# Moving the tiles that TensorE reads from 32 past a multiple of 64 bytes to a multiple of 64 bytes

## The chip, the cores and the metric

The kernel runs on one core of one Trainium2 chip. The metric is the device time of one execution in microseconds; the kernel before takes 1710.17 us, the median of three runs between 1709.99 and 1710.79. A core has TensorE (matrix products, from the on-chip memory SBUF into the accumulators PSUM), VectorE, ScalarE, GpSimd, and queues that start DMA transfers. SBUF has 128 partitions; a tile has an address (its first byte) that is the same in all of them.

## The reference

One layer of a hybrid encoder on 256 tokens of 2048 features, in float32. Cut to what matters:

```python
h = rms_norm(x, norm_mix_pre)
z = h @ w_in                                   # 2048 -> 14800 columns
o_conv, o_gla, o_diff, o_rwkv = four_mixers(z) # 512 features each
gates = sigmoid(z_gate)                        # four times 2048
merged = sum(gates[n] * (o[n] @ w_branch[n]) for n in range(4))
x = x + rms_norm(merged @ w_out, norm_mix_post)
h = rms_norm(x, norm_ffn_pre)
ffn = (silu(h @ w_gate) * (h @ w_up)) @ w_down # 5632 wide
x = x + rms_norm(ffn, norm_ffn_post)
```

## The kernel before

All large products are done in float32r, a float32 whose lower bits are rounded away, in three products that together keep the precision of float32: both operands are split into a rounded part `hi` and an exact remainder `lo`, and the sum is hi x hi + hi x lo + lo x hi.

Weights come in chunks of 256 rows by 512 columns, stored as [128, 2, 512], 0.5 MB each, in the order in which they are used. `Stream.chunk` (L578) issues the load into one of 4 slots `raw` of a ring (L583), lets ScalarE cast it to `hi` (L585) and VectorE subtract to `lo` (L586), each of which has 3 slots. The load of a chunk waits until the slot that it takes is free.

A product has a stationary operand, which is loaded into the array (its weight load is listed as PEld) and a moving operand, whose columns stream through it. Four kinds of loops make them:

- `gemm_tok` (L631, products at L646 to L648): the activations are stationary, 128 features by 128 tokens, and 512 columns of weights move. For each chunk 2 halves k, 2 token tiles i and 3 products: 12. The stationary tile is `hT_hi` or `hT_lo` (the input of the layer, L674, 16 blocks of 256 columns), `oT` (the output of a mixer, L748), `mT_hi`, `mT_lo` (the merged branches, L899) or `h2_hi`, `h2_lo` (the input of the feed-forward part, in the place of `hT`, L935; named `h_hi`, `h_lo` in the profile).
- `gemm_feat` (L654, products at L666 to L668): the weights are stationary, 128 columns of a chunk at a time, and 256 tokens of `hT` move. For each chunk 2 halves, 4 column tiles and 3 products: 24. The first projection (the low-rank parts) takes chunks of 464 columns in tiles that begin at column 0, 112, 208 and 336 and are 112, 96, 128 and 128 wide.
- the down projection (L1019 to L1026): as `gemm_tok`, with `ah` and `al` stationary, split from `aT` on the way (L1009 to L1014). For its last four chunks the split weights go to `wl`, which takes the place of `hT` once more (L1037).
- the mixers' own small products (RWKV, gated linear attention, differential attention) are in plain float32, as are the transposes (L1000 and others).

The order of the work on each engine is set by a scheduler from the program order and priorities; weights have a high priority.

Tiles are placed one behind the other in pools. A pool's tiles begin at a multiple of 32 bytes. The pool `base` holds small tables and the next pool, the ring, begins behind it. The built program places the tiles as follows (first byte; in brackets modulo 64 and modulo 512):

```
raw   19616 (32, 160) + 4096 n       hi  36000 (32, 160) + 4096 n      lo  48288 (32, 160) + 4096 n
hT_hi 60576 (32, 160)                hT_lo 76960 (32, 160)             h2, wl in the same place
oT    133088, 137184, 141280, 145376 (32, 480)
mT_hi 149472 (32, 480)               mT_lo 165856 (32, 480)
ah    191712 (32, 224) + 2048 n      al  197856 (32, 224) + 2048 n
```

The blocks within a tile are multiples of 512 bytes apart, so that a stationary block has its tile's place modulo 512. In `gemm_feat` the first projection's column tiles begin 0, 448, 832 and 1344 bytes into a half, which places them at 160, 96, 480 and 480 modulo 512. Tiles of the RWKV mixer are 4128 bytes apart (64 x 64 + 32), so that every second one is a multiple of 64: the product of L300 reads `KBT` and `W` both at 32 modulo 64 in its first two rounds over the sequence, and both at 0 in the third.

Of the kernel before, what the change touches and what calls it, by code (L numbers as in the profile page):

```python
# [6 lines left out]
F32 = mybir.dt.float32  # L7
F32R = mybir.dt.float32r
# [4 lines left out]
PSUM = bass.MemoryType.PSUM  # L13

# columns of the per-feature vector table
# [60 lines left out]
def rwkv_mixer(e, Zr, Zk, Zv, Zl, wa, g2, out_hi, out_lo):  # L76
    """Z*: [128, 4, 257] feature-major projections with a zero column in front."""
# [18 lines left out]
    # token shift  # L96
    zm = {}
    for q, (n, Z) in enumerate((("l", Zl), ("k", Zk), ("r", Zr), ("v", Zv))):
        t = m4("zm_" + n)
# [12 lines left out]
    # decay, in-context rate, gate  # L112
# [31 lines left out]
    # normalised key direction  # L144
# [22 lines left out]
    # k' = k (1 + (a - 1) k_a)  # L167
# [7 lines left out]
    # bonus  # L175
# [8 lines left out]
    # scaled operands, [b | k] and [a | r] side by side within a chunk  # L184
# [12 lines left out]
    # value, token-major, under the rows of sa  # L197
# [14 lines left out]
    # intra-chunk products, transposed: rows [b s | k s], columns [a t | r t]  # L212
# [17 lines left out]
    # N = (I - U)^-1 of the 32 strictly upper 64 x 64 blocks U = AM[b rows, a columns]  # L230
# [43 lines left out]
    # chunks  # L274
# [4 lines left out]
    for c in range(4):  # L279
# [8 lines left out]
        X = e.M.tile([128, 8, 64], F32, tag="X", name="X", bufs=2)  # rows of sa; of the output  # L288
# [23 lines left out]
        # group norm per head  # L312
# [36 lines left out]
def split_out(e, ps, gain, hi, lo):  # L349
    """hi + lo <- ps * gain (per partition), hi rounded to float32r."""  # L350
    e.nc.scalar.activation(hi, ps, AF.Copy, scale=gain)  # L351
    e.nc.vector.scalar_tensor_tensor(lo, ps, gain, hi.bitcast(F32), op0=ALU.mult, op1=ALU.subtract)


def head_norm_out(e, po, i, mul, ot, scale4):
    """ot[:, i] <- po / rms over each head of 128 (times mul, token-major)."""
    nc = e.nc
    V, S = nc.vector, nc.scalar
    sq = e.T_.tile([128, 512], F32, tag="hsq", name="hsq")
    # a square beyond float32 makes the mean infinite and rsqrt zero; scaled by 2^-8 it stays finite here  # L360
    V.tensor_scalar(sq, po, 2.0 ** 64, -(2.0 ** 64), op0=ALU.min, op1=ALU.max)
    S.activation(sq, sq, AF.Square, scale=2.0 ** -8)
    st = e.T_.tile([128, 4], F32, tag="hst", name="hst", bufs=2)
    ok = e.T_.tile([128, 4], F32, tag="hok", name="hok", bufs=2)
    V.tensor_reduce(st, sq.rearrange("p (h x) -> p h x", h=4), axis=AX.X, op=ALU.add)
    top = FMAX * 2.0 ** -16
    V.tensor_scalar(ok, st, top, None, op0=ALU.is_le)
    V.tensor_scalar(st, st, top, 2.0 ** 16 * scale4 / 128.0, op0=ALU.min, op1=ALU.mult)
    V.tensor_scalar(st, st, scale4 * 1e-5, None, op0=ALU.add)
    e.nc.gpsimd.tensor_tensor(st, st, e.mhalf.to_broadcast([128, 4]), op=ALU.pow)  # L370
    V.tensor_tensor(st, st, ok, op=ALU.mult)
    for h in range(4):
        s = slice(h * 128, (h + 1) * 128)
        if mul is not None:
            V.scalar_tensor_tensor(ot[:, i, s], po[:, s], st[:, h:h + 1], mul[:, i, s], op0=ALU.mult, op1=ALU.mult)
        else:
            S.activation(ot[:, i, s], po[:, s], AF.Copy, scale=st[:, h:h + 1])
# [14 lines left out]
def gla_mixer(e, q, k, wl, v, g, wa2, out_hi, out_lo):  # L392
    """q (scaled), k: [128, 2, 256] feature-major; wl: [16, 256]; v, g: [128, 2, 512] token-major."""
# [15 lines left out]
    # log(1 + x) = 2 atanh(x / (2 + x))  # L409
# [13 lines left out]
    # scores, transposed [s, t]: within a tile of 128 [hh, i, j], and from tile 0 to tile 1 [hh, j]  # L423
# [3 lines left out]
    # the diagonal: q . k of each token and head  # L427
# [12 lines left out]
    # pairs whose halves of a block of 2w differ, scaled about the middle of the block  # L440
# [59 lines left out]
def diff_mixer(e, q, k, v, lq, out_hi, out_lo):  # L500
    """q (scaled), k: [128 (map, d), 4 heads, 256] feature-major; v: [128, 2, 512]; lq: [128, 4, 64]."""
# [49 lines left out]
def conv_mixer(e, cu, b, rB, y, out_hi, out_lo):  # L551
    """cu: [128, 4, 258] (C * u behind two zero columns), b: two banks [128, 2, 256], rB [128, 256] their factor; y: [128, 4, 256] scratch."""
    nc = e.nc
    V, S = nc.vector, nc.scalar
    o = VCOL["conv"][0]
    for ft in range(4):
        w = [e.vec[:, o + 4 * j + ft:o + 4 * j + ft + 1] for j in range(3)]
        V.tensor_scalar(y[:, ft], cu[:, ft, 0:256], w[0], None, op0=ALU.mult)
        V.scalar_tensor_tensor(y[:, ft], cu[:, ft, 1:257], w[1], y[:, ft], op0=ALU.mult, op1=ALU.add)
        V.scalar_tensor_tensor(y[:, ft], cu[:, ft, 2:258], w[2], y[:, ft], op0=ALU.mult, op1=ALU.add)  # L560
    for p in range(2):
        V.tensor_tensor(y[:, 2 * p:2 * p + 2], y[:, 2 * p:2 * p + 2], b[p], op=ALU.mult)
        V.tensor_tensor(y[:, 2 * p:2 * p + 2], y[:, 2 * p:2 * p + 2], rB.unsqueeze(1).to_broadcast([128, 2, 256]), op=ALU.mult)
    S.copy(out_hi, y)
    V.tensor_tensor(out_lo, y, out_hi.bitcast(F32), op=ALU.subtract)


# blocks of 512 columns of w_in as chunks() of it holds them
# [3 lines left out]
class Stream:  # L572
    """Weights in: DMA -> (rounded part, exact remainder), both float32r."""
# [4 lines left out]
    def chunk(self, ap, w=512, into=None):  # L578
        """ap: [128, 2, w] in DRAM -> hi, lo [128, 2, w]."""
        e, nc = self.e, self.e.nc  # L580
        with e.tc.high_priority(offset=e.boost):
            raw = self.ring.tile([128, 2, 512], F32, tag="raw", name="raw", bufs=e.nraw)
            nc.sync.dma_start(raw[:, :, :w], ap)  # L583
            hi, lo = into or [self.ring.tile([128, 2, 512], F32R, tag=t, name=t, bufs=e.nhi) for t in ("hi", "lo")]
            nc.scalar.copy(hi[:, :, :w], raw[:, :, :w])  # L585
            nc.vector.tensor_tensor(lo[:, :, :w], raw[:, :, :w], hi[:, :, :w].bitcast(F32), op=ALU.subtract)  # L586
        return hi, lo


def hybrid_kernel(tc, x, xt, w_l, w_in, w_branch, w_out, w_gate, w_up, w_down, post_mix, post_ffn, wa2_d, w2_d, a2_d, g2_d, lq_d,  # L590
# [9 lines left out]
    with ExitStack() as ctx:  # L600
# [25 lines left out]
        def rms(ssum, n, eps):  # L626
            """ssum [128, 1] <- (ssum / n + eps) ** -0.5"""
            V.tensor_scalar(ssum, ssum, 1.0 / n, eps, op0=ALU.mult, op1=ALU.add)  # L628
            G.tensor_tensor(ssum, ssum, e.mhalf.to_broadcast(list(ssum.shape)), op=ALU.pow)  # L629

        def gemm_tok(w, lhs, nk, banks, pairs=()):  # L631
            """banks[i] [128 tokens, 512] <- lhs.T @ 512 columns; w(kc) -> [128, 2, 512], lhs(kt) -> (hi, lo) [128, 256].

            Token tile 0 goes through both chunks of a pair before token tile 1 does."""
# [19 lines left out]
        def gemm_feat(src, w, tiles, banks, before=None):  # L654
            """banks[j // 2][:, j % 2] [features, 256] <- (h @ w).T by column tiles (start, width) of the chunk."""
# [18 lines left out]
        hT_hi = hpool.tile([128, 16, 256], F32R, tag="hT_hi", name="hT_hi")  # L674
        hT_lo = hpool.tile([128, 16, 256], F32R, tag="hT_lo", name="hT_lo")
# [23 lines left out]
        def x_norm():  # L699
            """The norm's factor of each token: rst by partitions, rB along the free axis."""  # L700
# [23 lines left out]
        with ExitStack() as mctx:  # L724
# [22 lines left out]
            def out_pair(tag):  # L747
                return [PB.tile([128, 4, 256], F32R, tag=tag, name="oT", bufs=2) for _ in range(2)]  # L748
# [26 lines left out]
            oT_rwkv = out_pair("oR")  # L775
            with ExitStack() as rctx:
# [7 lines left out]
                # keeps the tensor engine at work until x is there  # L784
# [112 lines left out]
            L = mctx.enter_context(tc.tile_pool(name="L", bufs=1))  # L897
            tp = mctx.enter_context(tc.tile_pool(name="tp", bufs=1, space=PSUM))
            mT_hi = L.tile([128, 16, 256], F32R, name="mT_hi")  # L899
            mT_lo = L.tile([128, 16, 256], F32R, name="mT_lo")  # L900
# [9 lines left out]
            def merged(g):  # L910
                """Features g * 512.. of the gated sum."""
# [23 lines left out]
            h2_hi = hpool.tile([128, 16, 256], F32R, tag="hT_hi", name="h2_hi")  # L935
            h2_lo = hpool.tile([128, 16, 256], F32R, tag="hT_lo", name="h2_lo")
# [42 lines left out]
        with ExitStack() as fctx:  # L979
# [27 lines left out]
            for hf in range(2):  # L1007
                bk = [[(bank() if j == 0 else wd.tile([128, 512], F32, tag="wd", name="wd", bufs=4)) for i in range(2)] for j in range(2)]
                def activations(kc):  # L1009
                    ah = F.tile([128, 2, 256], F32R, tag="ah", name="ah", bufs=3)  # L1010
                    al = F.tile([128, 2, 256], F32R, tag="al", name="al", bufs=3)
# [23 lines left out]
                if hf == 1:  # L1035
                    # of the last four chunks token tile 0 is done first
                    wide = [hpool.tile([128, 16, 256], F32R, tag=t, name="wl").rearrange("p (c k x) n -> p c k (x n)", c=4, k=2)  # L1037
# [31 lines left out]
class TagPool:  # L1069
    """A pool whose tags have a fixed number of slots."""  # L1070
# [30 lines left out]
def chunks(w, n=512):  # L1101
    """[K, N] -> [K / 256, N / n, 128, 2, n]: the pieces that the kernel loads, each in one run."""
    k = w.shape[0]
    return w.reshape(k // 256, 2, 128, -1, n).transpose(0, 3, 2, 1, 4)
# [32 lines left out]
```

## Time and profile before

| what | us |
|---|---|
| runs: median (lowest, highest) | 1710.17 (1709.99, 1710.79) |
| span of the profiled execution, first to last instruction | 1707.7 |
| TensorE busy in it | 1665.4 |
| VectorE busy | 987.1 |
| ScalarE busy | 753.0 |
| 548 subtractions to `lo` on VectorE | 686.6 |
| 548 casts to `hi` on ScalarE | 575.7 |

The durations that the profile gives for products overlap: a product of 512 columns is listed with about 390 ns, and the next one starts before it ends. How fast TensorE goes is therefore read from the distance between starts, in the timeline or in the chain of work. The weight load of the next product starts 2 to 4 ns after a product does.

### The profile page before, as it was taken

The numbers are of one execution on the slowest core, as the hardware profiler recorded it, in microseconds if no ns is written. First come the engines' busy times: TensorE is split into PE (matmuls) and PEld (weight loads), VectorE is DVE, ScalarE is ACT, GpSimd is POOL, SyncE is SP. The second block draws the span as 40 slices with busy tenths as digits, with TensorE's granted clock in tenths as the row PEclk, the third lists the DMA queues.
The fourth block names the chain that finished last, engine by engine and source line by source line (L and its number), as shares of the span: only waits on it lengthen the run. The fifth ranks groups of instructions, "written<-read, shape, count | busy, mean of one in ns | idle before, by whom it ended". The sixth has DMA issues, their size and how long they took to land. (4 is left out here: it accounts for less than half of the span.)

```text
span 1707.7 us, 21846 instructions
## 1 busy us (share of the span) xinstructions
PE 1665.4 (98%) x8630; PEld 1402.6 (82%) x8630; DVE 987.1 (58%) x1040; ACT 753.0 (44%) x873; POOL 190.0 (11%) x168
## 2 busy tenths in 40 slices
PE   7999998999999999999999899999999999999997
PEld 6999976897788987888888788888888888888886
DVE  7667644669764458545554655445455554556555
ACT  3444342335544335544444644444444444445443
POOL 4005192111210001201000100000000000000001
PEclk8999998999999999999999999999999999999999
DMA  6654445445446554765555466565565555555653
GB/s 210 201 182 136 146 161 153 141 136 185 148 149 196 186 174 161 257 196 186 185 185 185 150 209 193 187 188 193 187 197 187 190 191 186 184 190 184 194 186 134
DMA packets 86087, 306.84 MB, mean 180 GB/s; under 512 B 9713, under 2 KB 12033, under 8 KB 85473
## 3 DMA queue, kind: packets, MB, share of 16 engines
q1 hardware_dynamic: 84208, 298.50, 54.4%
q0 software_dynamic: 1200, 5.90, 1.1%
q8 instruction: 67, 1.10, 0.3%
q10 hardware_dynamic: 576, 1.05, 0.2%
q14 instruction: 36, 0.29, 0.0%
HBM read 302.40 MB, written 3.01 MB: 179 GB/s over the span
## 5 line engine op out<-in xcount | busy, mean ns | idle before, releaser
L586 DVE TENSOR_TENSOR lo<-raw,hi 128x1024 fp32r<-128x1024 f32 (+1 forms) x556 | 699.2, 1259 | 597.3 <-ACT hi L585 596.6
L585 ACT CAST hi<-raw 128x1024 fp32r<-128x1024 f32 (+1 forms) x556 | 583.4, 1050 | 759.6 <-PE mm L648 532.4
L647 PE MATMUL mm<-lo,h_hi 128*128 128x512 f32 x704 | 275.0, 391 | 0.4 <-DVE lo L586 0.4
L648 PE MATMUL mm<-hi,h_lo 128*128 128x512 f32 x704 | 274.0, 390 | 0.0
L647 PE MATMUL mm<-lo,hT_hi 128*128 128x512 f32 x608 | 240.9, 396 | 13.3 <-DVE lo L586 13.2
L646 PE MATMUL mm<-hi,h_hi 128*128 128x512 f32 x704 | 250.2, 391 | 0.5 <-ACT h_hi L351 0.5
L648 PE MATMUL mm<-hi,hT_lo 128*128 128x512 f32 x608 | 238.9, 393 | 0.0
L646 PE MATMUL mm<-hi,hT_hi 128*128 128x512 f32 x608 | 221.7, 393 | 0.0
L668 PE MATMUL mm<-hT_hi,lo 128*128 128x256 f32 (+2 forms) x640 | 183.1, 289 | 10.3 <-DVE lo L586 10.3
L666 PE MATMUL mm<-hT_hi,hi 128*128 128x256 f32 (+1 forms) x640 | 185.2, 290 | 1.8 <-ACT hi L585 1.8
L667 PE MATMUL mm<-hT_lo,hi 128*128 128x256 f32 (+1 forms) x640 | 184.2, 289 | 0.0
L647 PEld LDWEIGHTS mm<-lo,h_hi 128*128 128x128 f32 x704 | 132.2, 188 | 28.0 <-DVE lo L586 0.9
L646 PEld LDWEIGHTS mm<-hi,h_hi 128*128 128x128 f32 x704 | 132.2, 188 | 27.8 <-ACT h_hi L351 0.7
L648 PEld LDWEIGHTS mm<-hi,h_lo 128*128 128x128 f32 x704 | 132.2, 188 | 27.0
L647 PEld LDWEIGHTS mm<-lo,hT_hi 128*128 128x128 f32 x608 | 114.8, 189 | 40.0 <-DVE lo L586 15.4
L646 PEld LDWEIGHTS mm<-hi,hT_hi 128*128 128x128 f32 x608 | 114.7, 189 | 24.4
L648 PEld LDWEIGHTS mm<-hi,hT_lo 128*128 128x128 f32 x608 | 114.8, 189 | 23.7 <-issue 0.3
L668 PEld LDWEIGHTS mm<-hT_hi,lo 128*128 128x128 f32 (+2 forms) x640 | 123.8, 194 | 11.5 <-DVE lo L586 11.2
L666 PEld LDWEIGHTS mm<-hT_hi,hi 128*128 128x128 f32 (+1 forms) x640 | 124.5, 194 | 3.2 <-ACT hi L585 2.2
L667 PEld LDWEIGHTS mm<-hT_lo,hi 128*128 128x128 f32 (+1 forms) x640 | 124.3, 194 | 1.1 <-issue 0.2
L629 POOL TENSOR_TENSOR s1f<-s1f,mhalf 128x1 f32<-128x1 f32 x2 | 1.1, 540 | 721.1 <-DVE s1f L628 721.1
L767 POOL TENSOR_TENSOR acc<-acc,gt 128x512 f32<-128x512 f32 x24 | 41.5, 1748 | 332.2 <-DVE gt L766 332.2
(351 smaller groups left out, 1892.5 us busy)
## 6 DMA issues: line engine op xcount, KB each, us to landing
raw<-in_w_in_dram SPq DMA_DIRECT2D x224, 512.0 KB, 3.5
raw<-in_w_gate_dram SPq DMA_DIRECT2D x88, 512.0 KB, 3.5
raw<-in_w_up_dram SPq DMA_DIRECT2D x88, 512.0 KB, 3.5
raw<-in_w_down_dram SPq DMA_DIRECT2D x88, 512.0 KB, 3.5
raw<-in_w_branch_dram SPq DMA_DIRECT2D x32, 512.0 KB, 3.5
raw<-in_w_out_dram SPq DMA_DIRECT2D x32, 512.0 KB, 3.5
raw<-in_w_l_dram SPq DMA_DIRECT2D x8, 464.0 KB, 5.8
xs<-in_x_dram POOLq DMA_DIRECT2D x1, 2048.0 KB, 12.9
```

The costliest lines, as they stand in the source:

```text
L585: nc.scalar.copy(hi[:, :, :w], raw[:, :, :w])
L586: nc.vector.tensor_tensor(lo[:, :, :w], raw[:, :, :w], hi[:, :, :w].bitcast(F32), op=ALU.subtract)
L629: G.tensor_tensor(ssum, ssum, e.mhalf.to_broadcast(list(ssum.shape)), op=ALU.pow)
L646: mm(banks[i_], ah[:, ts], hi[:, k, :], start=kt == 0, stop=False)
L647: mm(banks[i_], ah[:, ts], lo[:, k, :], start=False, stop=False)
L648: mm(banks[i_], al[:, ts], hi[:, k, :], start=False, stop=kt == nk - 1)
L666: mm(ps, hi[:, k, cs], hT_hi[:, kt, :], start=first, stop=False, skip_group_check=True)
L667: mm(ps, hi[:, k, cs], hT_lo[:, kt, :], start=False, stop=False, skip_group_check=True)
L668: mm(ps, lo[:, k, cs], hT_hi[:, kt, :], start=False, stop=last, skip_group_check=True)
L767: G.tensor_tensor(cs, cs, gt[:, i], op=ALU.add)
```

## The change

A constant `LINE = 64` is added, and the tiles below ask for a start at a multiple of it. Comments are taken out, and the lines from the import block on stand one further down. The instructions, their order on each engine, their shapes and their waits are the same.

```diff
+LINE = 64
...
-            raw = self.ring.tile([128, 2, 512], F32, tag="raw", name="raw", bufs=e.nraw)
+            raw = self.ring.tile([128, 2, 512], F32, tag="raw", name="raw", bufs=e.nraw, align_bytes=LINE)
...
-            hi, lo = into or [self.ring.tile([128, 2, 512], F32R, tag=t, name=t, bufs=e.nhi) for t in ("hi", "lo")]
+            hi, lo = into or [self.ring.tile([128, 2, 512], F32R, tag=t, name=t, bufs=e.nhi, align_bytes=LINE) for t in ("hi", "lo")]
...
-        hT_hi = hpool.tile([128, 16, 256], F32R, tag="hT_hi", name="hT_hi")
-        hT_lo = hpool.tile([128, 16, 256], F32R, tag="hT_lo", name="hT_lo")
+        hT_hi = hpool.tile([128, 16, 256], F32R, tag="hT_hi", name="hT_hi", align_bytes=LINE)
+        hT_lo = hpool.tile([128, 16, 256], F32R, tag="hT_lo", name="hT_lo", align_bytes=LINE)
...
-                return [PB.tile([128, 4, 256], F32R, tag=tag, name="oT", bufs=2) for _ in range(2)]
+                return [PB.tile([128, 4, 256], F32R, tag=tag, name="oT", bufs=2, align_bytes=LINE) for _ in range(2)]
```

`mT_hi`, `mT_lo`, `h2_hi`, `h2_lo`, `ah`, `al` and `wl` get the same argument. The built program then places the tiles so (first byte; in brackets modulo 64 and modulo 512):

```
raw   19648 (0, 192) + 4096 n        hi  36032 (0, 192) + 4096 n       lo  48384 (0, 256) + 4096 n
hT_hi 60672 (0, 256)                 hT_lo 77120 (0, 320)              h2, wl in the same place
oT    133248, 137344 (0, 128), 141504, 145600 (0, 192)
mT_hi 149696 (0, 192)                mT_lo 166144 (0, 256)
ah    191872 (0, 384) + 2048 n       al  198080 (0, 448) + 2048 n
```

## Rows read from the trace of the kernel before

**Rows 1.** The page, busy time: engine, us, share of the span, instructions

```profile
PE 1665.4 (98%) x8630; PEld 1402.6 (82%) x8630; DVE 987.1 (58%) x1040; ACT 753.0 (44%) x873; POOL 190.0 (11%) x168
```

**Rows 2.** Who waited for whom on TensorE: us in total, times, longest

```profile
PE mm L647 <- DVE lo L586: 13.7, 5, 10.3
PE mm L668 <- DVE lo L586: 10.3, 4, 5.5
```

**Rows 3.** The same for the load queue SPq

```profile
SPq L583 <- DVE lo L586: 1397.7, 542, 16.1
```

**Rows 4.** Groups by shape, whole span: count | busy us, mean ns | idle before us

```profile
L586 DVE TENSOR_TENSOR lo<-raw,hi 128x1024 fp32r<-128x1024 f32 x548 | 686.6, 1254 | 592.7 <-ACT hi L585 592.1
L585 ACT CAST hi<-raw 128x1024 fp32r<-128x1024 f32 x548 | 575.7, 1051 | 750.6 <-PE mm L648 532.4 <-PE mm L667 129.9 <-PE mm L1026 56.9
```

**Rows 5.** Groups by shape on TensorE, one of the three products each

```profile
L647 PE MATMUL mm<-lo,h_hi 128*128 128x512 f32 x704 | 275.0, 391 | 0.4 <-DVE lo L586 0.4
L647 PE MATMUL mm<-lo,hT_hi 128*128 128x512 f32 x608 | 240.9, 396 | 13.3 <-DVE lo L586 13.2
L1025 PE MATMUL mm<-lo,ah 128*128 128x512 f32 x168 | 66.2, 394 | 0.0
L1025 PE MATMUL mm<-wl,ah 128*128 128x512 f32 x8 | 3.2, 394 | 0.0
L647 PE MATMUL mm<-lo,mT_hi 128*128 128x512 f32 x128 | 50.7, 396 | 0.0
L667 PE MATMUL mm<-hT_lo,hi 128*128 128x256 f32 x608 | 174.2, 287 | 0.0
```

**Rows 6.** The chain of work, gate and up projections: start us, us, what

```profile
1055.77 0.66 PE tq L1000 x6
...
1100.22 0.66 PE tq L1000 x6
```

**Rows 7.** The chain of work, down projection

```profile
1459.85 0.47 PE wd L1024 x2
...
1465.45 0.47 PE wd L1024 x2
```

**Rows 8.** Timeline of TensorE, output projection: start us, us, instruction, count

```profile
885.29 0.63 PE L646 MATMUL mm<-hi,mT_hi 128*128 128x512 f32 x2
...
890.89 0.39 PE L646 MATMUL mm<-hi,mT_hi 128*128 128x512 f32 x1
```

**Rows 9.** Timeline of TensorE, a feature-major projection

```profile
150.00 0.28 PE L666 MATMUL mm<-hT_hi,hi 128*128 128x256 f32 x1
...
150.96 0.28 PE L668 MATMUL mm<-hT_hi,lo 128*128 128x256 f32 x1
```

**Rows 10.** Timeline of TensorE, the first projection at full clock

```profile
38.88 0.28 PE L666 MATMUL mm<-hT_hi,hi 128*128 128x256 f32 x1
...
39.90 0.28 PE L666 MATMUL mm<-hT_hi,hi 128*128 128x256 f32 x1
```

**Rows 11.** Timeline of TensorE, the first projection near the start

```profile
13.65 0.41 PE L666 MATMUL mm<-hT_hi,hi 128*128 128x256 f32 x1
...
14.29 0.41 PE L666 MATMUL mm<-hT_hi,hi 128*128 128x256 f32 x1
```

**Rows 12.** Stretches of TensorE: us, busy (count), granted clock, DMA share, GB/s

```profile
12.00:15.00 3.00, 3.00 (x16) 0.50 1.03 401
38.50:41.00 2.50, 2.50 (x24) 1.00 0.57 203
1056.50:1099.00 42.50, 42.50 (x189) 1.00 0.62 188
```

**Rows 13.** The page, what the DMA moved in 40 slices, GB/s

```profile
GB/s 210 201 182 136 146 161 153 141 136 185 148 149 196 186 174 161 257 196 186 185 185 185 150 209 193 187 188 193 187 197 187 190 191 186 184 190 184 194 186 134
```

**Rows 14.** Timeline of TensorE, float32 products of the RWKV mixer, two places

```profile
303.00 1.16 PE L300 MATMUL ps<-W,KBT 128*128 128x128 f32 x8
...
348.19 1.16 PE L300 MATMUL ps<-W,KBT 128*128 128x128 f32 x8
```

More of the change, by code (lines that the diff above doesn't have):

```diff
@@ L898, in hybrid_kernel @@
             tp = mctx.enter_context(tc.tile_pool(name="tp", bufs=1, space=PSUM))
-            mT_hi = L.tile([128, 16, 256], F32R, name="mT_hi")
-            mT_lo = L.tile([128, 16, 256], F32R, name="mT_lo")
+            mT_hi = L.tile([128, 16, 256], F32R, name="mT_hi", align_bytes=LINE)
+            mT_lo = L.tile([128, 16, 256], F32R, name="mT_lo", align_bytes=LINE)
             xs = L.tile([128, 2, 2048], F32, name="xs")
@@ L934, in hybrid_kernel @@
             x2 = acc
-            h2_hi = hpool.tile([128, 16, 256], F32R, tag="hT_hi", name="h2_hi")
-            h2_lo = hpool.tile([128, 16, 256], F32R, tag="hT_lo", name="h2_lo")
+            h2_hi = hpool.tile([128, 16, 256], F32R, tag="hT_hi", name="h2_hi", align_bytes=LINE)
+            h2_lo = hpool.tile([128, 16, 256], F32R, tag="hT_lo", name="h2_lo", align_bytes=LINE)
             def residual(g, i, pool):
@@ L1009, in activations @@
                 def activations(kc):
-                    ah = F.tile([128, 2, 256], F32R, tag="ah", name="ah", bufs=3)
-                    al = F.tile([128, 2, 256], F32R, tag="al", name="al", bufs=3)
+                    ah = F.tile([128, 2, 256], F32R, tag="ah", name="ah", bufs=3, align_bytes=LINE)
+                    al = F.tile([128, 2, 256], F32R, tag="al", name="al", bufs=3, align_bytes=LINE)
                     S.copy(ah, aT[:, 2 * kc:2 * kc + 2])
@@ L1035, in hybrid_kernel @@
                 if hf == 1:
-                    wide = [hpool.tile([128, 16, 256], F32R, tag=t, name="wl").rearrange("p (c k x) n -> p c k (x n)", c=4, k=2)
+                    wide = [hpool.tile([128, 16, 256], F32R, tag=t, name="wl", align_bytes=LINE).rearrange("p (c k x) n -> p c k (x n)", c=4, k=2)
                             for t in ("hT_hi", "hT_lo")]
```

## The prediction

> **What bounds the kernel now.** I read the share of busy time first, then who waited for whom, then the costliest groups by shape, and last the chain of work and the timeline, to get from how long an instruction lasts to how far apart two of them start. TensorE is busy 98% of a span of 1707.7 us, VectorE 58%, ScalarE 44% [rows 1]. TensorE's longest waits, 13.7 and 10.3 us in 5 and 4 places, are for the low halves of the weights that VectorE makes, and they lie at the start [rows 2]. Everywhere else the weights wait for TensorE: the queue that loads them stands 1397.7 us in total behind VectorE's release of a slot of the ring [rows 3], and the cast that makes a high half had 750.6 us of idle time before it, 532.4 of them ended by a product that gave a slot back; a chunk costs VectorE 1254 ns and ScalarE 1051 ns [rows 4], against about 2.7 us of TensorE for the 12 products of that chunk. So the time is the number of large products times the distance between their starts.
>
> The number: each of the three products of a split has as many as the row that stands for it, so there are 3 x (704 + 608) = 3936 products of 512 columns with `hT` or `h2` as stationary operand, 6 x (168 + 8) = 1056 of the down projection, and 3 x 128 = 384 each with `mT` and `oT`. Of 256 columns, with the weights stationary and `hT` moving, there are 3 x 608 = 1824 with 128 stationary columns [rows 5] and, by the loop over its four column tiles, 96 with 112 or 96; 192 of these 1920 belong to the first projection. That is 7680 in all.
>
> The distance is not the duration in those rows (390 ns), which overlaps the next product; it is read between starts. In the gate and up projections a group of 192 products and 8 transposes comes every 44.45 us [rows 6]; six of the transposes take 0.66 us there, 110 ns each, so a product has (44.45 - 0.88) / 192 = 226.9 ns; on the timeline the starts are 226 or 227 apart. In the down projection 24 products take 5.60 us, 233.3 ns each [rows 7], in the output projection also 5.60 us for 24 [rows 8]. In the feature-major products 8 take 0.96 us, 120 ns each [rows 9]; in the first projection, whose weights lie elsewhere in their slot, 9 take 1.02 us, 113.3 ns [rows 10].
>
> Against one column per cycle of 2.4 GHz (the granted clock is 1.00 in the stretches looked at [rows 12]), 213.3 ns for 512 columns and 106.7 for 256, these are too long by 13.3, 20, 20, 13.3 and 6.7 ns. Within the reading all are whole multiples of 6.67 ns, the time of 16 columns, and 16 columns of four bytes are 64 bytes. Near the start, while the granted clock is 0.50 (1.2 GHz) [rows 12], 3 products of 256 columns take 0.64 us, 213 ns each [rows 11]: one column per cycle with nothing on top. So the excess is not work of the array; it appears when the array asks for four bytes per partition every 0.42 ns, and it comes in pieces of 64 bytes. In all it is 3936 x 13.33 + 1824 x 20 + 1728 x 13.33 + 192 x 6.67 ns = 113.3 us, 7% of the span, and the operands' addresses are the only thing that differs between the 226.9 and the 233.3 ns (same shapes, same moving buffers).
>
> **The change, part by part.** It adds no instruction and moves none: the same instructions stand in the same order on each engine. What changes is where tiles start: the ring, `hT`, `h2`, `oT`, `mT`, `ah`, `al` and `wl` all start 32 bytes past a multiple of 64 before, and on a multiple after.
>
> *The products.* A moving operand of 512 columns is 2048 bytes: 32 pieces of 64 bytes if it starts on one, 33 if it starts half-way. If TensorE reads whole pieces of 64 bytes and can have one per 6.67 ns, the 33rd costs exactly one of the steps seen, 256 columns have 17 instead of 16 and pay the same step, and at 1.2 GHz, where a piece is due every 13.3 ns, the extra one is free. That is all three observations, and the smallest excess of any row, one step in [rows 10], is what the crossing alone would give. The second and third step are then meetings of the two streams (the weight load of the next product starts with a product and reads beside it), which depend on both addresses. I take one step per product for the change and leave the meetings as they are: 7680 x 6.67 ns = 51.2 us. From this goes what does not pay the step: the products at 1.2 GHz and those that stand behind a wait, about 250 by the starts on the timeline, 1.6 us. Sum: -49.6 us. Nothing becomes late behind it: a chunk would take TensorE 12 x 220 = 2.64 us, still twice VectorE's 1.25, and 0.5 MB in that time is 199 GB/s, where a slice of this trace holds 257 [rows 13].
>
> The bounds of that term. From above (no gain): the float32 products of the RWKV mixer have both kinds of address in this trace. Eight products of 128 columns take 1.16 us with both operands 32 past a multiple of 64 (at 303.00) and 1.16 us with both on a multiple (at 348.19) [rows 14]; so at that pace alignment is worth 0. They stream a column in two cycles, where a piece is due every 13.3 ns, so by the mechanism above they should show nothing, but they bound it at zero all the same. From below: all 113.3 us, or what is left of it if each product keeps the 3.3 ns that a transpose in [rows 6] has over 106.7 ns: 113.3 - 7680 x 3.3 ns = 88.0 us. I take the one step because the row nearest to it is [rows 10], the same products with one step of excess and no more.
>
> *Other users of the moved tiles.* ScalarE's casts, VectorE's subtractions and the loads into the ring touch the same tiles at the new addresses. They end ahead of TensorE by the waits of [rows 3, 4], so I cost them at nothing; if a cast and a subtraction each became 10% slower, a chunk would need 1.16 + 1.38 us in a row against 2.64, still hidden. The ring's growth moves all later tiles by 96 to 288 bytes, which swaps both kinds of address among the float32 tiles: 0 by [rows 14].
>
> The profiled execution's own time is the span of 1707.7 us; the median of the runs, 1710.17, is 2.5 us above it for what lies around. 1707.7 - 49.6 + 2.5 = 1660.6 us.
>
> **The Trainium skill against this.** Two alignments show one cost [rows 14]. The Trainium skill, SBUF — State Buffer, section Specifications (TRN2), gives lines of 16 bytes and asks for at least two hits in each; 32 past a multiple of 64 is a multiple of 16, and every operand here is contiguous. By that rule no operand crosses more lines after than before and the time stays 1710; whether a float32r operand at full pace obeys it no row shows, since none in this trace is aligned. It is the first rival below, which stands on [rows 14] without it.
>
> **Rivals.**
> *No change.* The step is fixed per product or depends on something else than the offset within 64 bytes. For it: [rows 14]. Against it: a fixed cost would not differ between [rows 9] and [rows 10], where a product has the same moving tiles and 128 stationary columns. Time 1710, within 0.2% (3.4 us, about what measurements of this kernel can tell from no change).
> *Slower: the streams meet more often.* What counts is the distance, modulo 512 bytes, from the moving tile to the stationary tile that is loaded beside it. Before, it is 0 for the 3936 products (226.9 ns), +64 in the down projection (233.3) and +320 in the output projection (233.3). The new addresses put the 3936 at +64, the output projection at 0, the down projection at +192, the feature-major products at -64. If the distance keeps its price and alignment gives nothing, the 3936 pay a step more, 26.2 us, and the 384 of the output projection one less, 2.6 us; the rest has no row (the 96-column products among [rows 10] lie at -64 and show 113.3, which would give back up to 12 us). 1722 to 1734 us. For it: it is the one reading in which the difference between [rows 6] and [rows 7] is explained by an address that is known. Against it: -192 in the output projection and in the 128-column products of [rows 10] is the same distance and has two more steps in the one than in the other. It decides as soon as alignment itself is worth less than half a step per product.
> *All excess goes.* The meetings come from the half pieces too and vanish with them: 1710.2 - 88.0 = 1622.2, or down to 1597 without the 3.3 ns. For it: no float32r row is free of the offset, so nothing shows that a meeting would remain. Against it: the excess varies by two steps between tiles that all have the same offset, so something else than the offset is at work.
>
> **How the numbers follow.** Forecast (one step of most products goes, the meetings add or take some): 53%, own range 1635 to 1690. No change: 17%. Slower by meetings: 18%. All excess goes: 12%. Faster than by 0.2%: 53 + 12 = 65%; within: 17%; slower: 18%. The range reaches from 1618, which holds about half of the fourth case, to 1718, which holds no change and the mild part of the slower case, and leaves out some 16%.
>
> **What would show it.** Right: the period of a gate group falls from 44.45 to 43.2 us (220 ns per product), 24 products of the down projection from 5.60 to 5.44, and the 256-column products from 120 to 113.3; the float32 products stay as they are; casts and subtractions keep their length. A period of 44.45 says no change; 45.7 in the gate groups with 120 or less in the feature-major ones says meetings; 41.9 to 42.5 says that all excess went. The forecast is wrong if the distances after are no multiples of 6.67 ns above 213.3, if the groups move in different directions, or if TensorE begins to wait for weights in mid-kernel.

## The result and the profile after

The changed kernel takes 1727.09 us (median of 4 runs, 1726.03 to 1728.61) against 1710.48 for the kernel before in the same series (4 runs): ratio 1.0095, 95% interval 1.0079 to 1.0110. It is 16.6 us slower, where 49.6 us less was forecast. The span of the profiled execution went from 1707.7 to 1724.6 us.

The page of the changed kernel, busy time (engine, us, share of the span, instructions):

```profile
PE 1683.8 (98%) x8630; PEld 1401.5 (81%) x8630; DVE 987.6 (57%) x1040; ACT 753.1 (44%) x873; POOL 189.8 (11%) x168
```

Beside [rows 1], TensorE is busy 18.4 us longer with as many instructions, and no other engine by more than 0.6 us. Who waited for whom on TensorE after the change (us in total, times, longest):

```profile
PE mm L648 <- DVE lo L587: 11.5, 4, 9.4
PE mm L669 <- DVE lo L587: 10.6, 4, 5.4
```

The same two waits as in [rows 2], 22.1 us together against 24.0: no new wait came in. The cast and the subtraction by shape (count | busy us, mean ns | idle before):

```profile
L587 DVE TENSOR_TENSOR lo<-raw,hi 128x1024 fp32r<-128x1024 f32 x548 | 686.9, 1254 | 609.0 <-ACT hi L586 608.3
...
L586 ACT CAST hi<-raw 128x1024 fp32r<-128x1024 f32 x548 | 575.1, 1050 | 762.9 <-PE mm L649 554.7 <-PE mm L668 130.9 <-PE mm L1027 55.9
```

1254 and 1050 ns against 1254 and 1051 [rows 4]; they only idle longer. So the products themselves come further apart. The chain of work of the changed kernel, gate and up projections (start us, us, what):

```profile
1109.11 0.66 PE tq L1001 x6
1154.79 0.66 PE tq L1001 x6
```

A group of 192 products takes 45.68 us against 44.45 [rows 6]: (45.68 - 0.88) / 192 = 233.3 ns per product instead of 226.9. Eleven groups of it are 13.5 us. The timeline of TensorE after the change, in five places (start us, us, instruction, count):

```profile
39.25 0.28 PE L668 MATMUL mm<-hT_lo,hi 128*128 128x256 f32 x1
...
40.20 0.28 PE L667 MATMUL mm<-hT_hi,hi 128*128 128x256 f32 x1
...
199.82 0.28 PE L667 MATMUL mm<-hT_hi,hi 128*128 128x256 f32 x1
...
200.88 0.28 PE L667 MATMUL mm<-hT_hi,hi 128*128 128x256 f32 x1
...
301.89 1.16 PE L301 MATMUL ps<-W,KBT 128*128 128x128 f32 x8
...
895.63 0.63 PE L647 MATMUL mm<-hi,mT_hi 128*128 128x512 f32 x2
...
898.39 0.62 PE L647 MATMUL mm<-hi,mT_hi 128*128 128x512 f32 x2
...
1500.49 0.62 PE L1025 MATMUL wd<-hi,ah 128*128 128x512 f32 x2
...
1506.06 0.62 PE L1025 MATMUL wd<-hi,ah 128*128 128x512 f32 x2
```

Read from start to start: the first projection has 8 products in 0.95 us, 118.8 ns, where it had 113.3 [rows 10]; a feature-major projection 9 in 1.06 us, 117.8 ns, where it had 120 [rows 9]; the float32 products stay at 1.16 us for eight [rows 14]; the output projection has 12 in 2.76 us, 230 ns, where it had 233.3 [rows 8]; the down projection 24 in 5.57 us, 232.1 ns, where it had 233.3 [rows 7]. The groups moved in different directions, which the prediction named as a sign that it is wrong.

Summed over the starts of all products in the two traces, each distance given to the product that it follows (us):

| products | number | before | after | difference |
|---|---|---|---|---|
| `h2` stationary | 2112 | 484.3 | 497.8 | +13.5 |
| `hT` stationary | 1824 | 439.2 | 447.4 | +8.2 |
| feature-major, first projection with them | 1920 | 252.2 | 249.4 | -2.8 |
| `ah`, `al` stationary | 1056 | 246.3 | 244.5 | -1.8 |
| `mT` stationary | 384 | 92.4 | 91.3 | -1.1 |
| `oT` stationary | 384 | 90.6 | 90.2 | -0.4 |
| float32 products and transposes | 950 | 91.4 | 92.5 | +1.1 |

The differences add up to +16.7 us, and the span grew by 16.9.

### The profile page after: what moved, and what is told of

It is laid out like the page before. It is cut to its first block, busy times and chain, and to the rows that moved or that the text cites. A ratio compares the mean times of both kernels' runs of the same rounds, so it can differ in the third digit from the quotient of the medians.

```text
span 1724.6 us, 21846 instructions
## 1 busy us (share of the span) xinstructions
PE 1683.8 (98%) x8630; PEld 1401.5 (81%) x8630; DVE 987.6 (57%) x1040; ACT 753.1 (44%) x873; POOL 189.8 (11%) x168
## 4 chain that ended last, share of the span: by engine, by line
PE 90%; POOL 3%; DVE 2%; issue 2%; DMA 1%; ACT 0%; DVEq 0%; SPq 0%; ACTq 0%; POOLq 0%
PE mm L648 20%; PE mm L647 20%; PE mm L649 20%; PE mm L669 4%; PE mm L667 4%; PE mm L668 4%; PE mm L1027 2%; PE mm L1026 2%; PE wd L1027 2%; PE mm L1025 2%; PE wd L1026 2%; PE wd L1025 2%; POOL tmp L245 1%; POOL NN L247 1%; DVE lo L587 1%
## 5 line engine op out<-in xcount | busy, mean ns | idle before, releaser
L648 PE MATMUL mm<-lo,h_hi 128*128 128x512 f32 x704 | 280.1, 398 | 0.0
L649 PE MATMUL mm<-hi,h_lo 128*128 128x512 f32 x704 | 277.8, 395 | 0.0
L647 PE MATMUL mm<-hi,h_hi 128*128 128x512 f32 x704 | 255.3, 398 | 0.5 <-ACT h_hi L352 0.5
```

Source lines behind the costliest of these rows:

```text
L647: mm(banks[i_], ah[:, ts], hi[:, k, :], start=kt == 0, stop=False)
L648: mm(banks[i_], ah[:, ts], lo[:, k, :], start=False, stop=False)
L649: mm(banks[i_], al[:, ts], hi[:, k, :], start=False, stop=kt == nk - 1)
```

## The experiments

The theory tested is the rival with which the prediction ended on the slow side: the distance from the moving to the stationary tile sets the spacing, and the alignment does nothing. Against it stand the prediction's own step (alignment saves 6.67 ns per product) and, later, other readings of "distance". All kernels are the kernel before with unused tiles as spacers, so that addresses move and instructions and their order do not; the last kernels also lengthen slots of the ring or put a spacer inside it. Distances are stationary minus moving, in bytes. A spacing given without a row is the mean from start to start over the products of a class (those with one kind of stationary tile) that follow one another without a wait; in the down projection it leaves out the last four chunks, whose weights `wl` lie elsewhere.

**Alignment alone.** All tiles of the change at a multiple of 64, all distances as before.

```diff
+        base.tile([128, 8], F32, name="pad_base")
         vec = base.tile([128, NVEC], F32, name="vec")
```

> All tiles 32 bytes further on, by one unused tile of 32 bytes in the first pool: every tile of the large products starts on a multiple of 64, and all distances between stationary and moving tiles are those of the kernel before. Theory D (only the distance modulo 512 counts): 226.9 ns per product of the gate and up projections, 233.3 in the down projection, 120 feature-major, and 1710 us. Theory A (the start on a multiple of 64 itself makes products slower): about 233 ns and 1727 us. Theory S (my forecast: a start on a multiple saves one step of 6.67 ns, and the new distances ate it): 220 ns in the gate and up projections and about 1660 us.

Measured: 1709.25 us (10 runs) against 1710.38 (13 runs), ratio 0.9997, interval 0.9988 to 1.0006. Its chain of work, gate and up projections:

```profile
1055.98 0.66 PE tq L1001 x6
1100.41 0.66 PE tq L1001 x6
```

44.43 us against 44.45. By the interval, alignment is worth at most 0.12% of 1710 us, 2.1 us or 0.27 ns on each of 7680 products, where the prediction had 6.67. This step falls. The Trainium skill, SBUF — State Buffer, section Specifications (TRN2), states lines of 16 bytes; by that rule a tile at 32 past a multiple of 64 touches no more lines than one on it, and the run agrees, with 0.27 ns at most.

**Distance alone.** The kernel before, nothing on a multiple of 64, with `hT` and `h2` 64 bytes further and all else at its old distance.

```diff
+        hpool.tile([128, 16], F32, name="pad_h")
         hT_hi = hpool.tile([128, 16, 256], F32R, tag="hT_hi", name="hT_hi")
```

(and 448 bytes ahead of `oT` and of `ah`, to keep their distances modulo 512.)

> The kernel before, all tiles still 32 past a multiple of 64, with 64 bytes of an unused tile ahead of hT: hT, h2 and wl alone lie 64 bytes further from the chunks; oT, mT, ah and al keep their distances. Theory D: the 3936 products with hT and h2 go from 226.9 to about 233.3 ns (+25 us), the feature-major ones from 120 to about 118 (-3 us), the rest stays; about 1732 us. Theory A: nothing changes, 1710 us. Theory S: +26 us as well, and above the changed kernel by the 50 us that alignment would have saved there, which cannot be, since that one is at 1727.

Measured: 1729.81 us (4 runs), ratio 1.0112, interval 1.0095 to 1.0129. Its chain in the same place:

```profile
1066.26 0.66 PE tq L1002 x6
1111.93 0.65 PE tq L1002 x6
```

45.67 us, the period of the changed kernel. The distance alone makes the whole slowdown. That the changed kernel takes 2.7 us less than this one is within the two intervals; its products with `oT`, `mT`, `ah` and `al`, which the change also moved, took 3.3 us less than before (table above).

**What each distance costs.** Two kernels with other multiples of 64, by five spacers each: `hT` and `h2` at 128 or 256; `oT` at 0 and 128, or 256 and 384; `mT` at 192 or 448; the down projection at 0 or 128.

```diff
+        hpool.tile([128, 32], F32, name="pad_h")
...
+            PB.tile([128, 16], F32, name="pad_R")
...
+            F.tile([128, 80], F32, name="pad_F")
```

> A map of distances, all tiles 32 past a multiple of 64: hT and h2 at +128, the first and third mixer outputs at 0, the other two at +128, mT at +192, ah and al at 0. Theory D: the down projection at distance 0 goes from 233.3 to 226.9 ns (-6.8 us), the same for the mixer outputs at 0; hT and h2, at +128, and the two mixer outputs at +128 show one and the same value, not known; mT at +192 about the 231.7 ns that the down projection has at +192 in the changed kernel. If the upper half of the memory has a price of its own (rival R), the down projection stays at 233.3 at distance 0.

> A second map, all tiles 32 past a multiple of 64: hT and h2 at +256, the first and third mixer outputs at +256, the other two at +384, mT at +448, ah and al at +128. Theory D: hT, h2 and the mixer outputs at +256 show one value; ah and al show what hT showed at +128 in the first map; 384 and 448 are not known. With rival R (the place in the memory counts) equal distances show different values in hT and in oT or ah.

Measured: 1716.13 and 1706.31 us (one run each). The chain of the first, down projection, which here has its activations at 0 from the chunk:

```profile
1472.92 0.45 PE wd L1029 x2
1478.36 0.45 PE wd L1029 x2
```

24 products in 5.44 us, 226.7 ns, against 5.60 [rows 7]: another tile, far from `h2` in memory, gets the price of `h2` once it has its distance. The chain of the second, gate and up projections, with `h2` at 256:

```profile
1052.64 0.66 PE tq L1004 x6
1097.07 0.66 PE tq L1004 x6
```

44.43 us, 226.8 ns per product, as at 0; the down projection at 128 shows 233.3, where `h2` at 128 shows 232.5. So the price goes by the distance modulo 256, within 1 ns, and not by the tile. One expectation missed: `mT` at 192 was to show the 231.7 ns of the down projection of the changed kernel and shows 228.9. In the changed kernel the low halves of the chunks lie 64 bytes further than the high ones, modulo 256, so that its products have not one distance; what that costs is the last question of this section.

Two readings settle one more rival, that the place of the stationary tile alone sets the price. In the run with alignment alone `h2`, in the place of `hT`, begins at byte 60608, and so it does in the first of the three kernels below (`h2` at 32); only the chunks lie 32 bytes further in the one than in the other, and a gate group takes 44.43 us in the one and 45.67 in the other. And in the run with distance alone, the moving weights `wl` of the last four chunks of the down projection (in the place of `hT`) came to the distance 0 from `ah` and `al`, which stayed at 224 modulo 512. The timeline of TensorE before, and of that run:

```profile
1690.22 0.39 PE L1024 MATMUL wd<-wl,ah 128*128 128x512 f32 x1
...
1693.02 0.39 PE L1025 MATMUL mm<-wl,ah 128*128 128x512 f32 x1
```

```profile
1713.90 0.39 PE L1028 MATMUL wd<-wl,ah 128*128 128x512 f32 x1
...
1716.62 0.39 PE L1029 MATMUL wd<-wl,al 128*128 128x512 f32 x1
```

12 products take 2.80 us before and 2.72 there, 233.3 and 226.7 ns.

Then three kernels at odd multiples of 32, again by spacers only, and at +192:

> The kernel before with unused tiles as spacers. Distance from the moving to the stationary tile: h2 and hT at +32 (feature-major products -32), the RWKV output at +96, the other outputs at +160, the merged branches at +224, the down projection at +96. Theory (the distance modulo 256 bytes alone sets the spacing, equally for all tiles): the output projection classes at +96 and the down projection at +96 show one and the same spacing, between 226.7 and 233.3 ns; h2 at +32 lies between the values at 0 (226.8) and at +64 (233.3); the time comes out between 1709 and 1731 us. Rival (only whole multiples of 64 count, the rest is rounded down): h2 at +32 as at 0, 226.8 ns, and the time 1705 to 1711 us. Rival (odd multiples of 32 avoid the meetings altogether): every class near 220 ns or below, 1665 us.

> The same with h2 and hT at +160 (feature-major -160, that is +96 modulo 256), the RWKV output at +224, the other outputs at +288, the merged branches at +352, the down projection at +416. Theory (distance modulo 256): the merged branches at +352 show what the down projection showed at +96 one run earlier, the down projection at +416 what h2 shows here at +160, the other outputs at +288 what h2 showed at +32; each within 1 ns. Rival (period 512 or a dependence on the tile itself): at least one of these pairs differs by 2 ns or more. Time 1709 to 1731 us by the theory, from 226.8 to 233.3 ns for 3936 products.

> The same with h2 and hT at +224 (feature-major +32), the RWKV output at +480, the other outputs at +32, the merged branches at +160, the down projection at +288. Theory (distance modulo 256): h2 at +224 equals the merged branches at +224 of the first of these three runs and the RWKV output at +480; the down projection at +288 equals the other outputs at +32; each within 1 ns. Between the values at +192 (228.9) and 256 (226.8) it would be about 228 ns, so that h2 and hT cost 3936 x 1 ns = 4 us more than before and the down projection at most 7 us less: 1705 to 1715 us. Rival (odd multiples of 32 are free of meetings): near 1665 us.

> The kernel before with two spacers: h2 and hT at +192, the feature-major products therefore at +64 modulo 256, output projection and merged branches at 0, down projection at +256. By the spacings measured so far: h2 and hT 3936 x 2.1 ns = 8.3 us more, the down projection 1056 x 6.6 = 7.0 us less, outputs and merged branches 768 x 6.5 = 5.0 us less; the feature-major products at +64 have no row of 128 columns after 128: if they show the 113.3 ns of the first projection, 1824 x 6.5 = 11.9 us less, together 1695 us; if they stay at 120, 1707 us. A rival in which the tile and not the distance sets the spacing leaves outputs and down projection at 233.3 ns: 1719 us.

Measured: 1729.38, 1730.32 and 1728.39 us (one run each), and 1702.14 us (4 runs, ratio 0.9950, interval 0.9934 to 0.9967). The chain of the first, with `h2` at 32:

```profile
1063.81 0.66 PE tq L1004 x6
1109.48 0.66 PE tq L1004 x6
```

45.67 us: 32 costs as much as 64. Both rivals of these runs (rounded down to 64, or free of meetings) fall, and so does my guess of 228 ns between the values at 192 and 256. The pairs that are equal modulo 256 agree within 0.3 ns (96, 96 and 352: 234.3 each; 32 and 288: 233.3, 233.1, 233.3, 233.3; 160 and 416: 233.4, 233.4, 233.3, 233.3). Over all runs in which the tiles of a class have one distance (the products with `hT`, which stand among the mixers' own work, show 227.4 to 227.7 at 0):

| distance modulo 256 | 0 | 32 | 64 | 96 | 128 | 160 | 192 | 224 |
|---|---|---|---|---|---|---|---|---|
| 512 columns move, ns | 226.7 to 226.9 | 233.1 to 233.3 | 233.3 | 234.3 | 232.5 to 233.3 | 233.4 | 228.9 | 233.3 |

For the feature-major products there is no such table, because one layout has several spacings. The timeline of the kernel with +192, two stretches of one kind of product with the same addresses modulo 512:

```profile
52.43 0.28 PE L666 MATMUL mm<-hT_hi,hi 128*128 128x256 f32 x1
...
54.70 0.28 PE L668 MATMUL mm<-hT_hi,lo 128*128 128x256 f32 x1
...
60.27 0.28 PE L667 MATMUL mm<-hT_lo,hi 128*128 128x256 f32 x1
...
62.63 0.28 PE L666 MATMUL mm<-hT_hi,hi 128*128 128x256 f32 x1
```

20 products in 2.27 us, 113.5 ns, and a little later 20 in 2.36, 118 ns. Stretches of each kind last for several chunks or many; which begins when, no run explains. The mean was 116.4 here, and the run came out at 1702, between the 1695 and 1707 of its two cases; the rival by which the tile sets the spacing (1719) falls too.

**The best layout.** First two spacers of 192 bytes, which put `oT`, `mT`, `ah` and `al` at 0 like `h2`; then, beside that, the high halves of the feature-major chunks 64 bytes further in slots that are 256 bytes longer.

```diff
+            PB.tile([128, 48], F32, name="pad_R")
             oT_rwkv = out_pair("oR")
...
             s1 = F.tile([128, 2], F32, name="s1f")
+            F.tile([128, 48], F32, name="pad_F")
```

```diff
-            hi, lo = into or [self.ring.tile([128, 2, 512], F32R, tag=t, name=t, bufs=e.nhi) for t in ("hi", "lo")]
+            hi, lo = into or (self.ring.tile([128, 1088], F32R, tag="hi", name="hi", bufs=e.nhi)[:, skew:skew + 1024]
+                              .rearrange("p (k n) -> p k n", k=2),
+                              self.ring.tile([128, 2, 512], F32R, tag="lo", name="lo", bufs=e.nhi))
...
-                hi, lo = stream.chunk(src(kc), w)
+                hi, lo = stream.chunk(src(kc), w, skew=16)
```

> The kernel before with two spacers of 192 bytes: outputs, merged branches and down projection at 0 modulo 256 like h2 and hT before; nothing else changes. Theory: 1056 x 6.6 + 768 x 6.5 = 12.0 us less, 1698.4 us; spacings 226.7 ns in all token-major classes, 120 in the feature-major products. Rival (places so near to each other in the bank that loads and evictions meet as well): some class above 227 ns, 1701 or more.

> The kernel before, with spacers that put the stationary tiles of all token-major products (h2, hT, outputs, merged branches, down projection) at 0 modulo 256 from the moving chunk, and with the high halves of the chunks of the feature-major products 64 bytes further in their slots (the low halves stay), so that two of each three feature-major products have a high half at +64 beside them and the third a low half at 0. Theory (the distance to the tile that is loaded beside sets the spacing): down projection 233.3 to 226.7, 1056 x 6.6 = 7.0 us less; outputs and merged branches 768 x 6.5 = 5.0 us less; h2 and hT as before; feature-major products between 116.4 (as at +64 throughout) and 120, about 117.6, 1824 x 2 = 4 us less: 1694 us, between 1690 and 1699. Rival (the skew of one half disturbs the rhythm of the three products): feature-major at 120 or above, 1698 us or more.

Measured: 1696.73 us (4 runs, ratio 0.9922, interval 0.9905 to 0.9939) and 1694.68 us (4 runs, ratio 0.9908, interval 0.9893 to 0.9923). The timeline of the first, output and down projection:

```profile
880.12 0.62 PE L646 MATMUL mm<-hi,mT_hi 128*128 128x512 f32 x2
...
885.57 0.62 PE L646 MATMUL mm<-hi,mT_hi 128*128 128x512 f32 x2
...
1480.27 0.62 PE L1026 MATMUL wd<-hi,ah 128*128 128x512 f32 x2
...
1485.71 0.62 PE L1026 MATMUL wd<-hi,ah 128*128 128x512 f32 x2
```

24 products in 5.45 and 5.44 us, 227 ns each, against 5.60 in [rows 7, 8]. The sum of 12.0 us was expected and 13.3 measured. The skew brought 2.05 us more, half of the 4 us expected: the feature-major mean fell to 118.2 ns. Both versions beat the kernel before and the changed one.

**Which distance.** The prediction spoke of the tile that is loaded beside a product, that of the product behind it. Three kernels shift the low halves by 64 bytes: the moving and the stationary one together, the stationary one alone, the moving one alone.

```diff
+                self.ring.tile([128, 16], F32, tag="pad", name="pad_lo", bufs=1)
                 lo = self.ring.tile([128, 2, 512], F32R, tag="lo", name="lo", bufs=e.nhi)
...
+        hpool.tile([128, 16], F32, name="pad_hlo")
         hT_lo = hpool.tile([128, 16, 256], F32R, tag="hT_lo", name="hT_lo")
```

> The kernel before with low halves, hT_lo and h2_lo each 64 bytes further against their high halves. The tile that is loaded during each h2 or hT product (that of the product behind it) stays at distance 0 from the moving chunk, while the product's own stationary tile, loaded before it, is at 0, -64 and +64 in turn. If the tile loaded beside counts: h2 stays at 226.8 ns in all three products. If the product's own tile counts: two of three go to 229 to 233 ns, the mean to about 230, and the time up by 10 to 18 us. The down projection and the merged branches have +64 for the high half and 0 for the low half beside: if each product has the price of its own distance, their mean is (2 x 233.3 + 226.7) / 3 = 231.1 ns. The time by the theory: 1710.4 less 1056 x 2.2 + 768 x 2.2 = 4 us, 1706.

> The kernel before with hT_lo and h2_lo alone 64 bytes further: the moving chunks hi and lo stay equal modulo 256. The tile loaded beside is at 0, +64, 0 for the products hi x h_hi, lo x h_hi, hi x h_lo; the product's own tile at 0, 0, +64. If the tile loaded beside counts, the second of the three is slow (233.3 against 226.8 ns); if its own tile counts, the third. In both cases the mean is 226.8 + 6.5 / 3 = 229 ns and the time 1710.4 + 3936 x 2.2 = 1719 us. If only the step between the two moving tiles made the slowdown of the run with the low halves shifted together, the mean stays at 226.8 ns and the time at 1710.

> The kernel before with the low halves lo of the chunks alone 64 bytes further; hT, h2 and their low halves stay equal modulo 256 with hi. The tile loaded beside is at 0, -64, 0 for the products hi x h_hi, lo x h_hi, hi x h_lo, and the product's own tile at 0, -64, 0 as well; -64 is +192 modulo 256, which cost 2.1 ns where all three had it. If the distance to either tile counts, the second is at 228.9 ns, the mean at 227.5 and the time at 1713 us; if the step between the moving tiles counts, the mean is that of the run with the low halves shifted together, 230.7 ns, and the time 1725 us or, with the lower price of down projection and merged branches there, 1721.

Measured: 1721.01, 1720.91 and 1725.50 us (one run each), with `h2` at 230.7, 230.7 and 232.6 ns on average. The timeline of the second, a stretch of the gate and up projections:

```profile
1100.32 0.62 PE L646 MATMUL mm<-hi,h_hi 128*128 128x512 f32 x2
1100.78 0.39 PE L647 MATMUL mm<-lo,h_hi 128*128 128x512 f32 x1
1101.01 0.39 PE L648 MATMUL mm<-hi,h_lo 128*128 128x512 f32 x1
1101.24 0.39 PE L647 MATMUL mm<-lo,h_hi 128*128 128x512 f32 x1
1101.47 0.40 PE L648 MATMUL mm<-hi,h_lo 128*128 128x512 f32 x1
1101.70 0.40 PE L646 MATMUL mm<-hi,h_hi 128*128 128x512 f32 x1
...
1103.09 0.62 PE L646 MATMUL mm<-hi,h_hi 128*128 128x512 f32 x2
```

12 products in 2.77 us, 230.8 ns, with single distances of 226 to 236. Over the whole stage the means behind hi x `h_hi`, lo x `h_hi` and hi x `h_lo` are 230.8, 229.6 and 231.7 ns, where either price per product asks for one at 233.3 and two at 226.8: no product of the three is the slow one here. In the down projection of the first run the three kinds do differ (235.4, 237.8 and 230.0 ns), and all are slower than at 0. The first run refutes that only the tile loaded beside counts, since that stayed at 0; the second refutes that only the step between moving tiles counts, since that stayed at 0 there; and none of the three keeps to a price per product (231.1 was expected in the down projection of the first and 234.4 measured, 229.0 for `h2` in the second, 227.5 or 230.7 in the third). The third meets the 1725 us of the 230.7 case, but not by that mean, so its time is luck. The first was expected at 1706 us and missed by 15. What holds is less: 226.7 to 226.9 ns was seen only where all tiles that follow one another agree modulo 256, and one odd tile among them costs 3.9 ns and more on average. How the streams meet inside stays open.

## Why the prediction was wrong

The step that failed is the first of the part on the products: one step of 6.67 ns per product for the piece of 64 bytes that an operand half-way between multiples touches in excess, 51.2 us in all. Alignment alone gave no measurable time (0.27 ns per product at most). The step stood on a count that fitted (all excesses are multiples of 6.67 ns), and the count would have fitted just as well without the 33rd piece (nor is it a law: 228.9 and 117.8 ns, measured since, are no whole number of steps above 213.3 and 106.7): no row had an aligned float32r operand at full pace, and the only aligned rows, [rows 14], said 0. They were set aside as too slow to show it.

The second half of that step failed too: the meetings of the two streams were left as they are. The prediction had seen that only addresses differ between 226.9 and 233.3 ns, in tiles that all lie 32 past a multiple of 64. That sentence alone rules alignment out as the cause of this difference and leaves the distance, which the change was going to alter for 3936 products. The rival that said so had the place, sign and size: a gate group of 45.7 us (45.68 measured) with 120 or less in the feature-major products (117.8), 26.2 us for the 3936 products (21.7 in the sums, since the 1824 with `hT` stood at 227.7 on average before, and the waits among them were 2.2 us shorter after), 1722 to 1734 us in all (1727.1). Its output projection, at 0, was to give back 2.6 us and gave 1.1: the low halves lie 64 bytes further there, and 230.6 ns is what `h2` shows in the run that shifts both low halves (230.7). It got 18% because of the argument against it, that one distance had two more steps in [rows 8] than in [rows 10]. That compared products of 512 columns with products of 256, and the latter have more than one spacing at one and the same distance, as the +192 run showed. The same rows made 113.3 ns the rival's best case for the feature-major products; they came to 117.8, which gave back 3 us and not 12.

What held: no instruction moved; no new wait came in; cast and subtraction kept their length; the float32 products of [rows 14] kept theirs (the 1.1 us more in the row of the table tells nothing: over all runs that row goes from 91.2 to 92.7 us); the chain stayed on TensorE. The first-projection value of 113.3, taken as nearest to the truth, was the floor of any row, and no layout reached it throughout. The rival of no change had the right cause for alignment, and would have been the result had only the alignment changed. That all excess goes has no run for it: no layout went under 226.7 ns.

## What to carry to other kernels

Where TensorE streams float32r without a gap, put the moving and the stationary tiles, high and low halves alike, at the same place modulo 256 bytes. No other kernel was tried; on this one two spacers of 192 bytes gave 0.8%, while rounding every address up to a multiple of 64 lost 1%. An alignment request is also a change of all distances behind it, so compare the addresses of tiles that are read together before and after, and not each by itself. When two groups of equal shape run at different paces, look for what differs between them and price the change by that, before explaining the part that they have in common.

## What the runs showed of the hardware

- The spacing of float32r products of 512 columns is 226.7 to 226.9 ns where moving and stationary tiles are equal modulo 256, 228.9 at 192 and 232.5 to 234.3 elsewhere, the same for `h2`, `oT`, `mT` and `ah` within 1 ns. The Trainium skill, SBUF — State Buffer, section Who interferes with whom, has the two reads of TensorE independent and TensorE waiting for nobody; read so, the distance between the two tiles could not matter, and here it makes 226.7 or 233.3 ns: the measurement decides.
- Whether operands begin at 0 or 32 modulo 64 bytes, at equal distances, makes less than 0.3 ns per product.
- Products of 256 columns keep a spacing for several chunks or many (113.5 and 118 ns at equal addresses modulo 512) and then change to another.
- The low stationary tile alone at 64 costs three fifths of what all of them cost there (230.7 against 226.8 and 233.3 ns), not a third; the low moving tile alone, which puts its own distance at 192, costs more than all of them at 192 (232.6 against 228.9).
